# Token-layout turns on VectorE block transposes and GpSimd transfers, in place of TensorE transposes

## The chip, the cores and the metric

The kernel runs on one core of one Trainium2 chip. The metric is the device time of one execution in microseconds (us), median over several runs. A profile of one execution, taken by the hardware profiler, stands beside it. The engines are called TensorE (PE in the profile; its weight loads are PEld), VectorE (DVE), ScalarE (ACT), GpSimd (POOL) and SyncE (SP). SP, ACT and POOL issue DMA transfers.

## What is computed

A decoder block on 512 tokens of width 2048, all in float32: an attention and linear-attention mixer, a cross-attention over 256 memory tokens, and a SwiGLU feed-forward part of inner width 5632. The change lies in the last part:

```
x = x + concat(o_nsa, o_gla) @ w_out
x = x + cross_attention(rms_norm(x), rms_norm(mem)) @ w_co        # this x is "x2" below
hf = rms_norm(x, g_ffn)
gg, uu = split(hf @ w_gu, 2)
return x + (silu(gg) * uu) @ w_down                               # h = silu(gg) * uu
```

## The kernel before

Each float32 operand is split into a high and a low part, and each product is three matmuls: high by high, low by high, high by low. A split of a tile is a cast on ScalarE (`qh`, or the high part in a `PB` tile) and a subtraction on VectorE (`ql`, or the low part), both at line 159. The large products also use a scheme with seven block products in place of eight, so that sums and differences of blocks are formed first.

**Gate and up projections.** They run over 11 column groups n = 0 to 10. For n of 1 and more there are two phases: phase 1 with four of the seven products (`PHASE_1`), phase 2 with three (`PHASE_2`). In each phase a loop over kp = 0 to 7 loads a block of `w_gu` into one of three `raw` buffers (issued by SP), forms differences on VectorE (lines 1282, 1284, 1293), splits, and multiplies. `kept[kp]` holds a block from phase 1 for phase 2; these eight tiles have the tag `T2`, which has eight buffers in all. The dictionary `extra` hangs other work behind a kp. After phase 1, VectorE adds results out of PSUM (lines 1475 to 1479); after phase 2 it does so again (lines 1501 and 1503) and forms the four tiles `hs` of h for this n (lines 1508 and 1510). For n = 10 these come right at the end of the phase.

**Turning h.** `hs` has tokens on the partitions; the down projection needs h columns on the partitions. `turn(hs, n - 1, k)` is hung behind kp 2 and kp 4 of phase 2 of the next n. It makes eight TensorE transposes of 128x128 into two PSUM banks (line 1380), two ScalarE copies out of them (1383, 1384), four VectorE sums (1386 to 1389) in T2 tiles, and four stores to the DRAM tensor `hd` issued by ScalarE (line 1394). The two turns of n = 10 run inside step 0 of the down projection, behind its kp 2 and 4. There are 22 turns.

**Down projection.** Four steps, `STEPS`, over 44 blocks kp of `w_down`; step 0 uses one of the seven products, each other step two. h comes back from `hd` in six groups g0 to g5 of up to 1024 columns: `load_h` (line 1537, issued by GpSimd) into a `PB` tile, then a split (ACT cast, VectorE subtraction, line 159 with `PB`). g0 to g3 for step 0 are asked for just ahead of it.

**Residual.** x2 lies in DRAM with its features on the partitions. `turn_x2` turns it in step 0: 64 TensorE transposes (line 1604) in eight groups, 64 ScalarE copies out of PSUM (line 1607), four loads of 1 MB into a `raw` buffer. The fence `issue_after(turned ...)` in `load_w` holds later weight splits behind those copies.

**Other transfers of GpSimd** in these stages are paced by TensorE: sums of quarters of `w_down` made by accumulating DMAs (`td` at lines 144 and 146, `tw` at lines 1426 and 1428).

The order on each engine is that of a scheduler: it takes the program's order with priorities (`AHEAD`, `EVICT`), so a change moves rows on engines that the diff doesn't touch. DMAs issued by GpSimd rotate over eight semaphores, so each also waits for the one eight before it (waits named DMASW in the rows below; DMAHW are those of SP and ACT).

Of the kernel before, what the change touches and what calls it, by code (L numbers as in the profile page):

```python
# [17 lines left out]
T = 512  # L18
# [42 lines left out]
def hybrid_block(ctx: ExitStack, tc: tile.TileContext, x_t, mem_t, sv, cmat, umask, w_a, w_r67, w_v, w_vg, w_v3,  # L61
# [26 lines left out]
    def bank(tag):  # L88
        return psp.tile([128, 512], F32, name=tag, tag=tag, bufs={"mm": 3, "s": 2, "t": 2, "o": 1}[tag])
# [1282 lines left out]
    hd = [dram.tile([128, 7 * 512 * len(g)], F32, name="h", tag=f"h{g[0]}", bufs=1) for g in GRP]

    def turn(hs, n, k, tag="s"):
        def go():
            ps = [bank(tag), bank(tag)]
            for f in range(2):
                c = 256 * k + 128 * f
                for i in range(NT):
                    PE.transpose(ps[f][:, 128 * i:128 * i + 128], hs[i][:, c:c + 128], ident)  # L1380

            e, o, a, b = [sb1("T2") for _ in range(4)]
            S.copy(e, ps[0])
            S.copy(o, ps[1])
            x, y = slice(0, 256), slice(256, 512)
            V.tensor_sub(a[:, x], e[:, y], o[:, y])
            V.tensor_sub(b[:, x], e[:, x], e[:, y])
            V.tensor_sub(a[:, y], a[:, x], e[:, x])
            V.tensor_add(b[:, y], o[:, x], a[:, y])
            d = hd[n // 2].rearrange("q (p c) -> q p c", p=7)  # L1390
            c = 512 * (n % 2) + 256 * k
            S.dma_start(d[:, 0, c:c + 256], e[:, x])
            for p, t in ((1, o), (3, a), (5, b)):
                S.dma_start(d[:, p:p + 2, c:c + 256], t.rearrange("q (p c) -> q p c", p=2))
        return go

# [40 lines left out]
    def late_sum():  # L1437
        return {kp: [sums.pop(0)] for kp in (3, 5)}

    rc2 = []  # L1440
    gate = []
    hs = None
    fence = ()
    for n in range(NB):
        if n == 0:
            b1, bp = first_banks
            u, c11 = [sb2("C") for _ in range(2)], [sb2("C") for _ in range(2)]
            with tc.high_priority(offset=2 * EVICT):
# [84 lines left out]
    def load_h(step, g):  # L1533
        n = 512 * len(GRP[g])
        for a in STEPS[step]:
            raw = h_raw[a, g] = sb2("PB")
            i = G.dma_start(raw[:, :n], hd[g][:, a * n:a * n + n])
# [13 lines left out]
    def load_w(step, kp):  # L1551

        with tc.high_priority(offset=AHEAD):
# [14 lines left out]
            with ExitStack() as behind:  # L1568
                if (step, kp - 3) in turned:
                    behind.enter_context(tc.issue_after(turned[step, kp - 3].ins))  # L1570
                w = [split_cols(raw, 0, 1024)]
                if step % 2 and (step, kp) not in tw:
                    V.tensor_add(y, x, y)
                w.append(split_cols(raw, 1024, 1024))
# [16 lines left out]
    res, turned = {}, {}

    def turn_x2(m, raw):
        b, j = m // 8, m % 8 // 4
        if m % 8 == 0:
            res[1, b] = [sb1("T2") for _ in range(4)]
            if b:
                res[0, b] = [sb2("C") for _ in range(4)]
            else:
                res[0, b] = [sb2("PA") for _ in range(4)]  # L1600
        ps = bank("t")
        for i in range(NT):
            c = 512 * (m % 4) + 128 * i
            PE.transpose(ps[:, 128 * i:128 * i + 128], raw[:, c:c + 128], ident)  # L1604
        for i in range(NT):
            c = 128 * (m % 4)
            copied = S.copy(res[i // 2, b][2 * (i % 2) + j][:, c:c + 128], ps[:, 128 * i:128 * i + 128])
        return copied
# [29 lines left out]
    for step, plan in enumerate(STEPS):  # L1638
# [9 lines left out]
        for kp in range(NK):  # L1648
# [11 lines left out]
            elif 1 < kp < NK - 2:  # L1660
                for r in rs_:
                    down_product(step, r, kp, range(4))
            if step == 0 and kp % 2 and 5 <= kp < 21:
                for m in (kp - 5, kp - 4):
                    if m % 4 == 0:
                        raw = sb1("raw")
                        nc.sync.dma_start(raw, x2d[m // 4])
                    turned[step, kp] = turn_x2(m, raw)
            if step == 0 and kp in (2, 4):
                turn(hs, NB - 1, kp // 2 - 1, "t")()  # L1670
            if step == 0 and kp in (5, 11):
                load_h(0, len(GRP) - (2 if kp == 5 else 1))
            if step < 3 and kp % 4 == 3:
# [139 lines left out]
```

## Time and profile before

| | |
|---|---|
| median of 3 runs | 2294.36 us (2292.84 to 2295.81) |
| span of the profiled execution | 2291.5 us (the page gives no other time for that execution) |
| TensorE busy | 2280.9 us, 100% |
| VectorE, ScalarE, GpSimd busy | 1661.9 us (73%), 1183.2 us (52%), 164.0 us (7%) |
| instructions | 29538 |
| DMA | 434.17 MB, mean 189 GB/s; queue q0 (GpSimd) 17.6%, q1 (SP) 39.9%, q10 (ACT) 3.5% of sixteen engines' span |

The stages that the change touches lie at these times of the span: the pairs of phases for n = 1 to 10 up to 1857.97 us, and step 0 of the down projection from there to about 1922 us. A share in the table is of the whole span; the stages differ from it.

### The profile page before, as it was taken

To read this page: it belongs to the slowest core of one execution; us is meant where nothing else is said; L and a number is where in the kernel's file an instruction comes from. 1 tells how busy PE (TensorE), PEld (TensorE's weight loads), DVE (VectorE), ACT (ScalarE), POOL (GpSimd) and SP (SyncE) were. 2 spreads that over 40 slices of the span, in tenths; PEclk is the share of its full clock that TensorE was granted. 3 is DMA by queue.
4 is the path that set the end of the run, shared out by engine and by line. 5 is a ranking of instruction groups with operands and counts; after the bars stand their busy time and mean duration, and the time that the engine had idled before them with its cause. 6 is when DMAs were issued, how large, how long until landed. Compare 5 with 4: busy or idle time off the path is not lost.

```text
span 2291.5 us, 29538 instructions
## 1 busy us (share of the span) xinstructions
PE 2280.9 (100%) x10773; PEld 1894.0 (83%) x10773; DVE 1661.9 (73%) x2555; ACT 1183.2 (52%) x1855; POOL 164.0 (7%) x240
## 2 busy tenths in 40 slices
PE   9999999999999999999999999999999999999999
PEld 8988888888888888787888888888888888888887
DVE  6478766677774446698788788888887875775685
ACT  6334545566774345675455445454554565444452
POOL 0012100011110000110000000000000000000000
PEclk9999999999999999999999999999999999999999
DMA  6577656466655343685556656565665598766754
GB/s 197 140 187 182 173 156 173 122 172 174 164 168 173 132 135 138 215 235 175 178 180 201 185 163 200 184 191 159 204 201 165 163 329 292 268 239 250 265 206 147
DMA packets 140593, 434.17 MB, mean 189 GB/s; under 512 B 14464, under 2 KB 35200, under 8 KB 136992
## 3 DMA queue, kind: packets, MB, share of 16 engines
q1 hardware_dynamic: 80752, 306.83, 39.9%
q0 software_dynamic: 33824, 96.75, 17.6%
q10 hardware_dynamic: 25872, 28.71, 3.5%
q8 instruction: 84, 1.38, 0.2%
q14 instruction: 61, 0.50, 0.1%
HBM read 390.81 MB, written 94.11 MB: 212 GB/s over the span
## 4 chain that ended last, share of the span: by engine, by line
PE 94%; DVE 2%; DMA 2%; ACT 1%; issue 1%; SPq 0%; DVEq 0%; ACTq 0%
PE mm L99 51%; PE t L99 17%; PE s L99 14%; PE o L99 10%; DMA w<-w_c 1%; PE t L817 1%; PE s L1380 1%; DVE wl L159 1%; DMA w<-w_vsw 0%; ACT wh L159 0%; PE t L1604 0%; DVE ql L159 0%; DMA w<-w_a 0%; PE t L1071 0%; DMA P<-w_v 0%
## 5 line engine op out<-in xcount | busy, mean ns | idle before, releaser
L159 ACT CAST qh<-raw 128x1024 fp32r<-128x1024 f32 (+1 forms) x526 | 509.4, 981 | 473.4 <-PE t L99 120.6
L159 DVE TENSOR_TENSOR ql<-raw,qh 128x1024 fp32r<-128x1024 f32 (+1 forms) x526 | 589.3, 1130 | 137.6 <-PE mm L99 45.5
L99 PE MATMUL mm<-X,wh 128*128 128x512 f32 x1600 | 504.2, 395 | 0.0
L99 PEld LDWEIGHTS mm<-X,wh 128*128 128x128 f32 x1600 | 294.0, 188 | 56.4 <-issue 0.8
L99 PE MATMUL t<-qh,PB 128*128 128x512 f32 x968 | 335.3, 391 | 0.0
L99 PE MATMUL mm<-X,wl 128*128 128x512 f32 x800 | 313.6, 392 | 0.1
L99 PE MATMUL mm<-qh,PB 128*128 128x512 f32 x868 | 309.9, 390 | 1.8 <-ACT qh L159 0.9
L159 DVE TENSOR_TENSOR wl<-w,wh 128x1024 fp32r<-128x1024 f32 (+2 forms) x150 | 179.7, 1200 | 153.7 <-ACT wh L159 151.7
L159 ACT CAST wh<-w 128x1024 fp32r<-128x1024 f32 (+2 forms) x150 | 154.2, 1029 | 239.0 <-PE mm L99 176.8
L99 PE MATMUL s<-qh,PB 128*128 128x512 f32 x672 | 232.8, 391 | 0.7 <-ACT qh L159 0.7
L99 PE MATMUL mm<-qh,PA 128*128 128x512 f32 x640 | 221.6, 389 | 0.0
L99 PEld LDWEIGHTS t<-qh,PB 128*128 128x128 f32 x968 | 181.8, 188 | 37.3
L99 PEld LDWEIGHTS mm<-qh,PB 128*128 128x128 f32 x868 | 162.9, 188 | 37.0 <-ACT qh L159 2.1
L99 PE MATMUL t<-ql,PB 128*128 128x512 f32 x484 | 188.5, 389 | 0.1
L99 PE MATMUL o<-qh,PB 128*128 128x512 f32 x484 | 187.5, 389 | 0.0
L99 PEld LDWEIGHTS mm<-X,wl 128*128 128x128 f32 x800 | 150.2, 188 | 32.6 <-DVE wl L159 1.4
L99 PE MATMUL mm<-ql,PB 128*128 128x512 f32 x434 | 169.3, 390 | 0.0
L99 PEld LDWEIGHTS s<-qh,PB 128*128 128x128 f32 x672 | 126.1, 188 | 26.7 <-ACT qh L159 1.1
L99 PEld LDWEIGHTS mm<-qh,PA 128*128 128x128 f32 x640 | 120.1, 188 | 25.2
L99 PE MATMUL s<-ql,PB 128*128 128x512 f32 x336 | 131.3, 391 | 0.1
L99 PE MATMUL mm<-ql,PA 128*128 128x512 f32 x320 | 124.5, 389 | 0.0
L1282 DVE TENSOR_TENSOR raw<-raw 128x1024 f32<-128x1024 f32 x80 | 97.4, 1218 | 36.4 <-DMA raw<-w_gu 36.4
(501 smaller groups left out, 3448.7 us busy)
## 6 DMA issues: line engine op xcount, KB each, us to landing
raw<-w_gu SPq DMA_DIRECT2D x88, 768.0 KB, 4.4
raw<-w_gu SPq DMA_DIRECT2D x88, 512.0 KB, 3.6
raw<-w_down SPq DMA_DIRECT2D x84, 512.0 KB, 5.1
td<-w_down POOLq DMA_DIRECT2D x66, 512.0 KB, 6.3
w<-w_a SPq DMA_DIRECT2D x60, 512.0 KB, 4.5
raw<-td SPq DMA_DIRECT2D x22, 1024.0 KB, 4.8
PB<-h POOLq DMA_DIRECT2D x35, 512.0 KB, 5.9
h<-T ACTq DMA_DIRECT2D x66, 256.0 KB, 3.8
```

Source lines behind the costliest of these rows:

```text
L99: last_mm[0] = PE.matmul(*args, **kw)
L159: return S.copy(hi, src), V.tensor_sub(lo, src, hi)
L817: PE.transpose(tp[:, 128 * (i - j):128 * (i - j) + 128], ps_[b][:, POFF[i] + 128 * j:POFF[i] + 128 * j + 128], ident)
L1282: V.tensor_sub(raw[:, 0:1024], raw[:, 0:1024], raw[:, 512:1536])
L1380: PE.transpose(ps[f][:, 128 * i:128 * i + 128], hs[i][:, c:c + 128], ident)
```

## The change

1. **h is turned without TensorE.** `turn` returns two functions. `go` makes, on VectorE, four transposes of 32x32 blocks (one instruction each, 128 partitions by 8 blocks of 32) and the same four sums. Since only the inside of each 32x32 block is turned, the blocks still have to be moved to their places; `put` does that with sixteen GpSimd DMAs into `hd`, whose pieces are 64 elements (256 bytes) long. `go` hangs behind kp 2 and 4 of phase 2, `put` behind kp 3 and 5; both follow in step 0 for n = 10. The two PSUM banks and copies and the ACT stores are gone.
2. **x2 is turned ahead of the down projection.** `x2_turn` does it in 16 tiles of 128x512, one in a phase: `x2_load` (GpSimd, into the only buffer of tag `hT`) and, behind kp 6, `x2_blocks` (one VectorE block transpose in place); `x2_store` (four GpSimd DMAs of 32x16x32 in pieces of 128 bytes, into the new DRAM tensor `x2n`) comes in the next phase behind kp 2, ahead of the next load. In step 0, `load_x2` takes it back with 64 SP loads of 32x512. `turn_x2`, its 64 transposes and its 64 copies are gone, and so is the fence in `load_w`.
3. **Token order.** Block transposes give the tokens another order, and the output rows come in it; they are put in order outside of the device time.

```diff
-    def turn(hs, n, k, tag="s"):
+    def x2_load(m):
+            x2_tiles[m] = sb2("hT")
+            G.dma_start(x2_tiles[m], x2d[m // 4][:, 512 * (m % 4):512 * (m % 4) + 512])
+    def x2_blocks(m):
+            V.transpose(x2_tiles[m], x2_tiles[m])
+    def x2_store(m):
+            rows = x2n.rearrange("(b r) f -> r b f", r=32)
+            for a in range(4):
+                p = slice(32 * a, 32 * a + 32)
+                c = 128 * m + 32 * a
+                G.dma_start(rows[:, :, c:c + 32], x2_tiles[m][p].rearrange("r (b c) -> r b c", c=32))
+    def turn(hs, n, k):
         def go():
-            ps = [bank(tag), bank(tag)]
-            for f in range(2):
-                c = 256 * k + 128 * f
-                for i in range(NT):
-                    PE.transpose(ps[f][:, 128 * i:128 * i + 128], hs[i][:, c:c + 128], ident)
-            e, o, a, b = [sb1("T2") for _ in range(4)]
-            S.copy(e, ps[0])
-            S.copy(o, ps[1])
+            x, y, a, b = [sb1("T2") for _ in range(4)]
+            for i in range(NT):
+                to = (x, y)[i // 2].rearrange("q (g i c) -> q g i c", i=2, c=32)
+                V.transpose(to[:, :, i % 2], hs[i][:, 256 * k:256 * k + 256].rearrange("q (g c) -> q g c", c=32))
...
-            S.dma_start(d[:, 0, c:c + 256], e[:, x])
-            for p, t in ((1, o), (3, a), (5, b)):
-                S.dma_start(d[:, p:p + 2, c:c + 256], t.rearrange("q (p c) -> q p c", p=2))
+        def put():
+            for q in range(4):
+                p = slice(32 * q, 32 * q + 32)
+                d = hd[n // 2].rearrange("(g r) c -> r g c", r=32)[:, :, c + 64 * q:c + 64 * q + 64]
+                G.dma_start(d[:, 8:12], y[p, 256:].rearrange("r (g c) -> r g c", c=64))
+                for i, z in ((0, x), (12, a), (20, b)):
+                    G.dma_start(d[:, i:i + 8], z[p].rearrange("r (g c) -> r g c", c=64))
+        return go, put
...
+    def x2_turn(extra):
+        m = next(turns, None)
+        if m is not None:
+            if m:
+                extra.setdefault(2, []).append(x2_store(m - 1))
+            if m < KT:
+                extra.setdefault(2, []).append(x2_load(m))
+                extra.setdefault(6, []).append(x2_blocks(m))
...
-            extra = {2: [turn(hs, n - 1, 0)], 4: [turn(hs, n - 1, 1)], 6: [lambda: gate.append(last_mm[0])]}
+            (go0, put0), (go1, put1) = [turn(hs, n - 1, k) for k in range(2)]
+            extra = {2: [go0], 3: [put0], 4: [go1], 5: [put1], 6: [lambda: gate.append(last_mm[0])]}
...
-            if step == 0 and kp % 2 and 5 <= kp < 21:
-                for m in (kp - 5, kp - 4):
-                    if m % 4 == 0:
-                        raw = sb1("raw")
-                        nc.sync.dma_start(raw, x2d[m // 4])
-                    turned[step, kp] = turn_x2(m, raw)
+            if step == 0 and kp in (6, 8, 10, 12):
+                load_x2(*((0, 1), (1, 1), (0, 0), (1, 0))[kp // 2 - 3])
             if step == 0 and kp in (2, 4):
-                turn(hs, NB - 1, kp // 2 - 1, "t")()
+                go, put = turn(hs, NB - 1, kp // 2 - 1)
+                go()
+                put()
```

The scheduler moves rows at three places. In the rows, numbers behind a name are buffers, and square brackets hold the semaphores that the row waits for.

**VectorE at the seam between phase 2 of n = 10 and step 0.** Before, the split of g0 (the row with `PB_16128`, the low part of g0) stands in the middle of phase 2, ahead of the sums (L1386) of the turn of n = 9:

```order
L159 TENSOR_TENSOR ql_15944<-raw_15936,qh_15943 128x512 [waits PE_49,Activation_49]
L1293 TENSOR_TENSOR raw_16018<-raw_16018,T2_15706 128x512 [waits DMAHW6_49,DVE_49]
L159 TENSOR_TENSOR ql_15969<-raw_15965,qh_15968 128x1024 [waits PE_49,Activation_49]
L159 TENSOR_TENSOR PB_16128<-PB_16125,PB_16127 128x1024 [waits DMASW4_49,Activation_49]
L159 TENSOR_TENSOR ql_15973<-raw_15965,qh_15972 128x512 [waits DVE_49,PE_49]
L1293 TENSOR_TENSOR raw_16047<-raw_16047,T2_15745 128x512 [waits DMAHW7_49,DVE_49]
L1386 TENSOR_TENSOR T2_15924<-T2_15922,T2_15923 128x256 [waits Activation_49]
L159 TENSOR_TENSOR ql_16022<-raw_16018,qh_16021 128x1024 [waits PE_49]
```

After, both turns of n = 10 stand at the seam, and the split of g0 (`PB_16321`) comes behind them, with that of g1 (`PB_16327`) next:

```order
L1408 TENSOR_TENSOR T2_16402<-T2_16402,T2_16400 128x256 [waits DVE_49]
L1404 STREAM_TRANSPOSE T2_16475<-C_16298 128x8x32 [waits DMASW4_49,DMASW0_49]
L1409 TENSOR_TENSOR T2_16403<-T2_16400,T2_16402 128x256 [waits DVE_49]
L1404 STREAM_TRANSPOSE T2_16475<-C_16299 128x8x32
L1404 STREAM_TRANSPOSE T2_16476<-C_16300 128x8x32 [waits DMASW5_49,DMASW1_49]
L1404 STREAM_TRANSPOSE T2_16476<-C_16301 128x8x32
L1406 TENSOR_TENSOR T2_16477<-T2_16476 128x256 [waits DMASW6_49,DMASW2_49,DVE_49]
L1408 TENSOR_TENSOR T2_16477<-T2_16477,T2_16475 128x256 [waits DVE_49]
L1407 TENSOR_TENSOR T2_16478<-T2_16475,T2_16476 128x256 [waits DMASW7_49,DMASW3_49]
L1409 TENSOR_TENSOR T2_16478<-T2_16475,T2_16477 128x256 [waits DVE_49]
L159 TENSOR_TENSOR PB_16321<-PB_16318,PB_16320 128x1024 [waits DMASW4_49,Activation_49]
L159 TENSOR_TENSOR PB_16327<-PB_16324,PB_16326 128x1024 [waits DMASW0_49,Activation_49]
```

The split of g0 moved from phase 2 to behind all of phase 2's results, the four rows that form `hs`, and the eight transposes and eight sums of n = 10's turns.

**GpSimd at the same seam.** Before, the loads of g0 to g3 follow the last `td` sum:

```order
L146 DMA td_93<-w_down 128x1024 [waits PE_49]
L144 DMA td_93<-td_93 128x2x512 [waits DMASW3_49,DMASW2_49,PE_49]
L1537 DMA PB_16125<-h_8854 128x1024 [waits DMAHW3_49,DMAHW4_49,PE_49,Pool_49]
L1537 DMA PB_16131<-h_8855 128x1024 [waits DMAHW3_49,DMAHW4_49,DMASW5_49,PE_49]
L1537 DMA PB_16137<-h_8856 128x1024 [waits DMAHW3_49,DMASW4_49,DMAHW4_49,DVE_49,PE_49]
L1537 DMA PB_16143<-h_8857 128x1024 [waits DMAHW3_49,DMASW7_49,DMAHW4_49,DMASW5_49,DVE_49]
```

After, the load of g0 (`PB_16318`) comes behind the 32 transfers of `put` of n = 9's turns, the last of which are the first five rows here, and the loads of g1 and on stand between those of n = 10:

```order
L1420 DMA h_8858<-T2_16186 32x8x64 [waits DMASW7_49]
L1418 DMA h_8858<-T2_16184 32x4x64 [waits DMASW0_49]
L1420 DMA h_8858<-T2_16183 32x8x64 [waits DMASW1_49]
L1420 DMA h_8858<-T2_16185 32x8x64 [waits DMASW2_49]
L1420 DMA h_8858<-T2_16186 32x8x64 [waits DMASW3_49]
L1576 DMA PB_16318<-h_8854 128x1024 [waits DMASW4_49,PE_49,Pool_49]
L1418 DMA h_8859<-T2_16401 32x4x64 [waits DMASW5_49,DVE_49]
L1420 DMA h_8859<-T2_16400 32x8x64 [waits DMASW6_49]
L1420 DMA h_8859<-T2_16402 32x8x64 [waits DMASW7_49,DVE_49]
L1576 DMA PB_16324<-h_8855 128x1024 [waits DMASW0_49,PE_49]
L1420 DMA h_8859<-T2_16403 32x8x64 [waits DMASW1_49,DVE_49]
```

The loads of h moved behind the puts, and share their eight semaphores.

**VectorE and GpSimd between phase 1 and phase 2 of a middle group.** Before, VectorE goes from the splits of phase 2's first block straight to the additions out of PSUM (L1475):

```order
L1293 TENSOR_TENSOR raw_10222<-raw_10222,T2_9915 128x512 [waits DMAHW2_49]
L159 TENSOR_TENSOR ql_10215<-raw_10211,qh_10214 128x1024 [waits PE_49,Activation_49]
L159 TENSOR_TENSOR ql_10219<-raw_10211,qh_10218 128x512 [waits PE_49,Activation_49]
L1475 TENSOR_TENSOR C_10199<-C_10199,s_9887 128x512 [waits PE_49,Activation_49]
L159 TENSOR_TENSOR ql_10226<-raw_10222,qh_10225 128x1024 [waits DVE_49,PE_49]
L1475 TENSOR_TENSOR C_10200<-C_10200,s_9888 128x512 [waits PE_49,Activation_49]
L1477 TENSOR_TENSOR C_10201<-C_10199,t_9889 128x512 [waits DVE_49,PE_49]
L1477 TENSOR_TENSOR C_10202<-C_10200,t_9890 128x512 [waits DVE_49,PE_49]
```

After, the block transpose of the second x2 tile of the pair (`hT_10964`) stands ahead of them (now L1513):

```order
L1404 STREAM_TRANSPOSE T2_10949<-C_10514 128x8x32 [waits DVE_49]
L1404 STREAM_TRANSPOSE T2_10949<-C_10515 128x8x32
L159 TENSOR_TENSOR ql_10865<-raw_10861,qh_10864 128x1024 [waits PE_49,Activation_49]
L159 TENSOR_TENSOR ql_10869<-raw_10861,qh_10868 128x512 [waits PE_49,Activation_49]
L1384 STREAM_TRANSPOSE hT_10964<-hT_10964 128x512 [waits DMASW3_49,DMASW2_49,DMASW6_49,DMASW1_49,DMASW0_49]
L1513 TENSOR_TENSOR C_10849<-C_10849,s_10530 128x512 [waits PE_49,Activation_49]
L159 TENSOR_TENSOR ql_10876<-raw_10872,qh_10875 128x1024 [waits DVE_49,PE_49]
L1513 TENSOR_TENSOR C_10850<-C_10850,s_10531 128x512 [waits PE_49,Activation_49]
L1515 TENSOR_TENSOR C_10851<-C_10849,t_10532 128x512 [waits DVE_49,PE_49]
```

On GpSimd, that tile's load stands behind the four stores of the tile before it (`hT_10654`, the same single buffer), a `td` sum, and the first transfer of a put, which itself waits for VectorE (the transposes `T2_10949` above):

```order
L1379 DMA hT_10654<-x2_8866 128x512 [waits DMAHW0_49,DMASW5_49]
L1452 DMA tw_9400<-w_down 256x512 [waits DMASW6_49,DMASW4_49]
L146 DMA td_85<-w_down 128x1024 [waits DMASW7_49,PE_49]
L1393 DMA x2n_8860<-hT_10654 32x16x32 [waits DMASW0_49,DVE_49]
L1393 DMA x2n_8860<-hT_10654 32x16x32 [waits DMASW1_49]
L1393 DMA x2n_8860<-hT_10654 32x16x32 [waits DMASW2_49]
L1393 DMA x2n_8860<-hT_10654 32x16x32 [waits DMASW3_49]
L144 DMA td_85<-td_85 128x2x512 [waits DMASW7_49,PE_49]
L1418 DMA h_8854<-T2_10949 32x4x64 [waits DMASW5_49,DVE_49]
L1379 DMA hT_10964<-x2_8866 128x512 [waits DMASW3_49,DMASW6_49,DMASW2_49,DMAHW3_49,DMASW1_49,DMASW0_49]
L1420 DMA h_8854<-T2_10948 32x8x64
```

Nothing of this stood on GpSimd in these phases before but the rows of `td` and `tw`.

More of the change, by code (lines that the diff above doesn't have):

```diff
@@ L1371, in hybrid_block @@
     GRP = [range(g, min(g + 2, NB)) for g in range(0, NB, 2)]
[L1372 to L1374 removed]
+    hd = [dram.tile([7 * 128, 512 * len(g)], F32, name="h", tag=f"h{g[0]}", bufs=1) for g in GRP]
+    x2n = dram.tile([T, D], F32, name="x2n", tag="x2n", bufs=1)
+    x2_tiles = {}
+    def x2_load(m):
         def go():
[L1376 to L1395 removed]
@@ new lines, in turn, with go @@
+    def turn(hs, n, k):
+        t = []
+        def go():
+            x, y, a, b = [sb1("T2") for _ in range(4)]
+            for i in range(NT):
+                to = (x, y)[i // 2].rearrange("q (g i c) -> q g i c", i=2, c=32)
+                V.transpose(to[:, :, i % 2], hs[i][:, 256 * k:256 * k + 256].rearrange("q (g c) -> q g c", c=32))
+            e, o = slice(0, 256), slice(256, 512)
+            V.tensor_sub(a[:, e], y[:, e], y[:, o])
+            V.tensor_sub(b[:, e], x[:, e], y[:, e])
+            V.tensor_sub(a[:, o], a[:, e], x[:, e])
+            V.tensor_add(b[:, o], x[:, o], a[:, o])
+            t.extend((x, y, a, b))
+        def put():
+            x, y, a, b = t
+            c = 512 * (n % 2) + 256 * k
+            for q in range(4):
[5 more added lines that the diff above has]
+        return go, put
@@ L1438, in late_sum @@
         return {kp: [sums.pop(0)] for kp in (3, 5)}
+    turns = iter(range(KT + 1))
+    def x2_turn(extra):
[6 more added lines that the diff above has]
+                extra.setdefault(6, []).append(x2_blocks(m))
+        return extra
     rc2 = []
@@ L1493, in hybrid_block @@
         else:
-            phase(lambda kp: weights_2(n, kp), (b1, b2, b3), PHASE_2, (1, 0, 2), (0, 1, 2), False, AHEAD, extra,
-                  (fa, fv))
+            phase(lambda kp: weights_2(n, kp), (b1, b2, b3), PHASE_2, (1, 0, 2), (0, 1, 2), False, AHEAD,
+                  x2_turn(extra), (fa, fv))
         g1, g2 = [sb2("C") for _ in range(2)], [sb2("C") for _ in range(2)]
@@ L1536, in load_h @@
             raw = h_raw[a, g] = sb2("PB")
-            i = G.dma_start(raw[:, :n], hd[g][:, a * n:a * n + n])
+            i = G.dma_start(raw[:, :n], hd[g][128 * a:128 * a + 128])
             if step == 0 and g in (2, 3):
@@ L1567, in load_w @@
                 nc.sync.dma_start(y, tw.get((3, kp), td[kp][:, 1024:]))
[L1568 to L1574, printed above, removed]
+            w = [split_cols(raw, 0, 1024)]
+            if step % 2 and (step, kp) not in tw:
+                V.tensor_add(y, x, y)
+            w.append(split_cols(raw, 1024, 1024))
             if step == 2:
@@ L1588, in down_product, with load_x2 @@
                 start=fresh and kp == 0, stop=kp == NK - 1, again=not fresh)
[L1591 to L1608, printed above, removed]
+    res = {}
+    def load_x2(a, b):
+        res[a, b] = [sb1("T2") if a else sb2("C" if b else "PA") for _ in quad]
+        for (i, j), t in zip(quad, res[a, b]):
+            for q in range(4):
+                r, c = 256 * a + 64 * i + 32 * (q // 2) + 128 * (q % 2), 1024 * b + 512 * j
+                nc.sync.dma_start(t[32 * q:32 * q + 32], x2n[r:r + 32, c:c + 512])
     def store(x, a, b):
@@ L1811 @@
     r = run_bass_kernel_spmd(nc, [arrays], core_ids=[0])
-    return r.results[0]["out_0_dram"].reshape(1, T, D)
+    y = r.results[0]["out_0_dram"].reshape(2, 2, 2, 2, 32, D)
+    return y.transpose(0, 3, 1, 2, 4, 5).reshape(1, T, D)
```

12 lines of the change are left out of this document (9 added, 3 removed).

## The prediction

> **What bounds the kernel now.** I read the engine shares first, then the clock row and the chain of work that ended last.
>
> ```profile
> PE 2280.9 (100%) x10773; PEld 1894.0 (83%) x10773; DVE 1661.9 (73%) x2555; ACT 1183.2 (52%) x1855; POOL 164.0 (7%) x240
> PEclk9999999999999999999999999999999999999999
> PE 94%; DVE 2%; DMA 2%; ACT 1%; issue 1%; SPq 0%; DVEq 0%; ACTq 0%
> ```
>
> TensorE is busy for the whole span and its granted clock is full in every slice. The waits of TensorE say how close its suppliers come. The longest wait:
>
> ```profile
> PE t L99 <- DVE ones_r L229: 1.5, 1, 1.5
> ```
>
> So whatever leaves TensorE shortens the run, as long as no supplier becomes late; and whatever makes a supplier late lengthens it one for one. The forecast is a gain on TensorE less the new lateness. Everything is summed on the profiled span of 2291.5 us, which is 2.9 below the median of 2294.36; I carry the difference over to the median.
>
> **What leaves TensorE.** One group of eight transposes in TensorE's timeline (start, duration, then the work):
>
> ```profile
> 1131.72 0.39 PE L99 MATMUL o<-qh,PB 128*128 128x512 f32 x1
> 1131.95 1.03 PE L1380 MATMUL s<-ident,C 128*128 128x128 f32 x8
> 1132.74 0.48 PE L99 MATMUL t<-qh,PB 128*128 128x512 f32 x1
> 1133.06 0.40 PE L99 MATMUL t<-ql,PB 128*128 128x512 f32 x1
> ```
>
> Durations overlap, so starts count. Matmuls start 0.23 apart (1131.72, 1131.95). The group holds TensorE from 1131.95 to 1132.74, 0.79 us, and the matmul behind it takes 0.32 instead of 0.23: 0.88 a group. The counts:
>
> ```profile
> L1380 PE MATMUL s<-ident,C x160: 270/272/273, 1132.0 to 1845.6; 128*128 128x128 f32 x160
> L1380 PE MATMUL t<-ident,C x16: 270/272/273, 1866.1 to 1873.2; 128*128 128x128 f32 x16
> L1604 PE MATMUL t<-ident,raw x64: 270/273/273, 1876.1 to 1921.3; 128*128 128x128 f32 x64
> ```
>
> 240 transposes are 30 groups: 30 x 0.88 = **26.4 us** of gain, 17.6 in the gate-up phases and 8.8 in step 0. With them go ScalarE's copies and stores; ScalarE is 52% busy, so I cost that at nothing.
>
> The Trainium skill, "VectorE: DVE Perf Modes", section "The three transpose paths", gives 390 ns for a TensorE transpose of 128x128 in bf16 and 311 for VectorE's. The row shows 0.79 us for eight, about 0.1 each once pipelined, so that by the page's 390 the removal would be worth 240 x 0.39 = 94 us; the trace decides for 26.4.
>
> **Loss 1: the first split of step 0.** VectorE's order after the change puts the split of g0 behind the end of phase 2, the rows that form h, and both turns of n = 10. TensorE's third matmul of step 0 needs that split. Before:
>
> ```profile
> 1837.23 1.23 DVE L159 TENSOR_TENSOR PB<-PB 128x1024 fp32r<-128x1024 f32 x1 [1.97 <-ACT PB L159]
> ...
> 1859.06 0.68 DVE L1503 TENSOR_TENSOR C<-C,o 128x512 f32<-128x512 f32 x1
> 1859.66 1.22 DVE L159 TENSOR_TENSOR ql<-raw,qh 128x1024 fp32r<-128x1024 f32 x1
> 1860.80 1.41 DVE L1508 SCALAR_TENSOR_TENSOR C<-C,rc 128x512 f32<-128x512 f32 x2
> 1862.12 0.74 DVE L1510 SCALAR_TENSOR_TENSOR C<-C,rc 128x512 f32<-128x512 f32 x1
> ...
> 1871.01 0.42 DVE L1386 TENSOR_TENSOR T<-T,T 128x256 f32<-128x256 f32 x1 [1.01 <-ACT T L1384]
> 1871.36 0.42 DVE L1387 TENSOR_TENSOR T<-T 128x256 f32<-128x256 f32 x1
> 1871.69 0.42 DVE L1388 TENSOR_TENSOR T<-T,T 128x256 f32<-128x256 f32 x1
> 1872.14 0.42 DVE L1389 TENSOR_TENSOR T<-T,T 128x256 f32<-128x256 f32 x1
> ```
>
> ```profile
> 1857.97 0.39 PE L99 MATMUL s<-qh,PB 128*128 128x512 f32 x1
> 1858.19 0.39 PE L99 MATMUL s<-ql,PB 128*128 128x512 f32 x1
> 1858.42 0.62 PE L99 MATMUL s<-qh,PB 128*128 128x512 f32 x2
> ```
>
> Before, the split ran at 1837.23, 21 us ahead of its use. Now count from 1857.97, where TensorE leaves phase 2. VectorE ends the additions at 1859.66 (+1.69), one `ql` (+1.14), four rows forming h at 0.66 (+2.64), then eight transposes and eight sums of 128x256. The trace has no block transpose; the nearest row of its size, a sum of 128x256, starts 0.34 apart, 0.45 where it needs the one before (1871.69 to 1872.14). Lower end 0.2 each, upper 0.66 (the 128x512 row); I take the sum's own 0.34, with some waits: 16 x 0.34 + 4 x 0.11 = 5.9. Then the split, 1.14. Together 1.69 + 1.14 + 2.64 + 5.9 + 1.14 = 12.5 after 1857.97, and TensorE stands from 0.45 on: **12.0 us** lost, with ends of 11 and 14.6 (transposes at 0.2 or 0.66). Here more than the saving in step 0 (8.8) is lost. What is queued behind the wait is only the rest of step 0; weights are loaded in the meantime, so nothing else becomes late. The load of g0 itself stands on GpSimd behind a put of 16, and would have to be over 10 us later than phase 2's end to decide.
>
> A wait of 12 us is eight times the longest that TensorE had, so no row here shows the clock after one. The Trainium skill, "TensorE: Matmul & The Clock Gate", section "What's actually happening", states half rate for about 3.4 us after an idle window of that length; by the page the sum would be 1.7 us longer, which is inside the range.
>
> **Loss 2: the x2 tiles between phases 1 and 2.** For n of about 2 to 8 the second tile's transpose stands ahead of the additions that free PSUM for phase 2:
>
> ```profile
> 1183.07 0.68 DVE L1293 TENSOR_TENSOR raw<-raw,T 128x512 f32<-128x512 f32 x1
> 1188.48 0.69 DVE L1293 TENSOR_TENSOR raw<-raw,T 128x512 f32<-128x512 f32 x1 [2.46 <-DMA raw<-w_gu]
> 1194.72 0.69 DVE L1475 TENSOR_TENSOR C<-C,s 128x512 f32<-128x512 f32 x1 [1.57 <-ACT C L1474]
> 1197.06 1.28 DVE L1477 TENSOR_TENSOR C<-C,t 128x512 f32<-128x512 f32 x2
> ```
>
> ```profile
> 1200.57 0.39 PE L99 MATMUL t<-qh,PB 128*128 128x512 f32 x1
> ```
>
> The last addition for `t` ends at 1198.3 and is needed at 1200.57; with the rows between, the transpose must be over by about 1197.3. The first tile's transpose runs behind L1293 of 1183.07, to 1184.5. Then GpSimd issues four stores, each of 512 pieces; the last must have landed before the one `hT` buffer is loaded again, and the load must land. Durations of issues, and times to landing (a store of `spill`, and a 128x512 load `PA<-x`):
>
> ```profile
> L144 POOL DMA_DIRECT2D td<-td x22 | 26.0, 1184 | 163.1 <-PE s L99 93.1 <-PE mm L99 57.6 <-issue 12.4
> L1428 POOL DMA_DIRECT2D tw<-w_down x8 | 4.1, 514 | 288.0 <-PE o L99 288.0
> L1537 POOL DMA_DIRECT2D PB<-h x42 | 22.4, 535 | 324.6 <-PE mm L99 141.7 <-DVE PB L159 52.6 <-PE t L99 44.7
> ```
>
> ```profile
> DMA to landing us min/median/max: 2.4/4.8/7.9
> ```
>
> ```profile
> DMA to landing us min/median/max: 3.2/4.6/6.6
> ```
>
> An issue of 128 pieces takes 0.535, the `td` row of 256 pieces 1.18. For 512 pieces: 0.54 if pieces don't matter, 2.46 on a line through both rows. I take 1.18, the row that also has a three-dimensional pattern. Last store issued at 1184.5 + 3 x 1.18 = 1188.0, landed 1192.8, load landed 1197.4, transposed (0.65) 1198.05: 0.75 late. With 0.54: not late. With 2.46: last store 1191.9, landed 1196.7, load landed 1201.3, done 1202: 4.7 late. Times seven pairs: **0, 5 or 33 us**; I take 5.
>
> **Loss 3: transfers.** A pair gets 7168 pieces of 256 bytes (two puts, 3584 each) and 4096 of 128 (eight stores), and loses the ACT stores, 1920 packets.
>
> ```profile
> q10 hardware_dynamic: 25872, 28.71, 3.5%
> ```
>
> ```profile
> 1154.10:1197.60 43.50, 43.50 (x193) 35.80 (x192) 36.01 (x41) 21.98 (x28) 1.72 (x2) 1.00 0.58 178
> 1197.60:1232.00 34.40, 34.40 (x161) 28.64 (x160) 26.06 (x38) 15.93 (x21) 1.67 (x2) 1.00 0.57 189
> 1280.00:1358.00 78.00, 78.00 (x354) 64.71 (x353) 63.53 (x80) 39.18 (x50) 3.13 (x4) 1.00 0.61 186
> 1230.00:1235.00 5.00, 4.35 (x19) 3.30 (x19) 5.00 (x8) 3.71 (x6) 0.98 (x1) 1.00 1.00 231
> ```
>
> The ACT queue's packets of 1.1 KB cost 3.5% of 16 x 2291.5 over 25872, 49.6 ns. At that price per piece the pair gains (11264 - 1920) x 0.0496 / 16 = 29 us per DMA engine, and the share of 0.58 (last but one column; the rows are phase 1, phase 2, a whole pair and a crowded stretch, with the window, TensorE, its loads, VectorE, ScalarE, GpSimd, clock, share and GB/s) goes to 0.96; by bytes (11.4 and 5.7 ns) it stays where it is. In between, at 30 and 25 ns: share 0.76. The last row shows what fullness costs: at share 1.00 TensorE stood 0.65 of 5 us. I take a fifth of a microsecond to 0.4 a pair, **2 us** for eight pairs; ends 0 and 10 (two such places a pair). VectorE gets 8 x 0.34 + 2 x 0.6, 4 us more a pair on 36.01 of 43.5 and 26.06 of 34.4; it stays under its limit, so this costs nothing beyond the places named.
>
> The Trainium skill, "DMA: Bandwidth & Descriptors", section "Why small descriptors are slow (HBM only)", counts 256/32 + 3 = 11 cycles for a piece of 256 bytes, a quarter of it overhead; by the page loss 3 would vanish, as by bytes. No row here has such pieces in number.
>
> **The sum.** -26.4 + 12.0 + 5 + 2 = -7.4; on the median 2294.36 - 7.4 = **2287 us**. The bound for telling a change of this kernel is 0.2%, 4.6 us: faster is under 2289.8, slower over 2298.9.
>
> **The rivals.**
> - *Short waits.* VectorE turns at 0.2 a piece, stores are issued at 0.54, small pieces go by bytes: losses 11 + 0 + 0, and 2294.4 - 15.4 = 2279. For it: the flat 0.51 to 0.54 of most GpSimd issues. Should the seam cost less than counted, by VectorE working ahead, down to 2270. Chance 0.22.
> - *The single hT buffer holds up every pair.* It ends on the other side: at 2.46 a store, 4.7 x 7 = 33 in place of 5, so 2315. It decides from a store issue of about 1.9, where the sum turns to loss over 0.2%. For it: 1184 against 535 as pieces double. Against: the accumulating rows, of which that one is, may be dearer for another reason. Chance 0.17.
> - *Full DMA engines.* Pieces at 49.6 ns, share 0.96: weights late at two or more places a pair, 10 to 20 us: -7.4 + 13 = +6, 2300. For it: the 0.65 at share 1.00. Chance 0.13.
> - *Nothing is saved*, since other waits fill TensorE's place: that needs suppliers with no slack, and TensorE's waits are under 1.5 us; 0.03, near 2294.
>
> The likeliest case, the sum, has 0.45 and reaches from 2280 to 2297: two thirds faster than 0.2%, the rest same. Faster: 0.22 + 0.29 = 0.51; slower: 0.17 + 0.10 = 0.27 and a little of the sum's, 0.28; same 0.21. The range takes in short waits from 2273 and the single buffer to 2316.
>
> **What would show it.** Lines 1380 and 1604 gone, and TensorE busy some 26 us less. A wait of TensorE at the start of step 0 of about 12 us on `PB` from VectorE, the longest in its list. At the seams of seven pairs, a wait on `C` of under 1 us, and VectorE's idle time ahead of L1384 put down to `hT`'s load. GpSimd's issue at L1393 near 1.2 us decides between the sum and the single buffer; DMA share in the pairs near 0.75 between the sum and full engines. I would be wrong if the seam wait is under 8 us, or if any pair takes longer than its 78 us.

## The result: slower, by what looked like a rival

The changed kernel takes 2315.36 us (median of 4 runs, 2314.8 to 2319.99) against 2294.06 before: 21.3 us more. The ratio as estimated from all runs is 1.0099, interval 1.0084 to 1.0113; the two medians alone give 1.0093. The forecast was 2287 and faster. The profiled execution took 2314.8, its span is 2313.0, 21.5 over that of before. (A detail of the text above: a step of the down projection has 22 kp, not 44.)

The page of the changed kernel, with the engine row, the clock row and the DMA queue of GpSimd:

```profile
PE 2270.6 (98%) x10533; PEld 1870.0 (81%) x10533; DVE 1697.6 (73%) x2659; ACT 1152.6 (50%) x1747; POOL 417.8 (18%) x672
PEclk9999999999999999999999999999999989999999
q0 software_dynamic: 48416, 125.35, 21.7%
```

The 240 transposes are gone (10773 to 10533), but TensorE now idles 42.4 us of its span in place of 10.6. Its waits, by line:

```profile
PE mm L99 <- DVE ql L159: 9.9, 6, 2.2
PE s L99 <- DVE PB L159: 8.7, 2, 8.2
PE s L99 <- ACT qh L159: 6.1, 7, 1.1
PE s L99 <- ACT PB L159: 5.0, 2, 2.9
PE t L99 <- DVE ql L159: 2.9, 6, 0.5
```

None of the five was there before but 0.7 of the third. By stage (from the first matmul of phase 2 of one n to that of the next, read in TensorE's timeline; the column of both_sp belongs to an experiment below):

| | before | after | both_sp |
|---|---|---|---|
| phase 2 of n = 1 to that of n = 2 | 78.1 | 76.9 | 76.3 |
| the next seven pairs, one by one | 79.3, 78.0, 78.0, 78.4, 78.0, 78.0, 78.0 | 81.9, 80.7, 79.6, 81.1, 80.5, 80.2, 80.6 | 76.2 to 76.7 |
| n = 9 to n = 10 | 78.0 | 76.8 | 76.2 |
| from step 0's start to the end | 433.5 | 442.3 | 433.7 |

Two pairs gained 1.2 to 1.3 us of the 1.8 that their transposes cost. Seven pairs that should have come down to 76.2 went to 80.7 in the mean: 7 x 4.5 = 31 us lost. From step 0 on, 8.8 us should have gone and 8.8 came: 17.6 lost. Together -26.4 + 31 + 17.6 = 22, against 21.5 measured.

**A seam of such a pair.** GpSimd and VectorE of the changed kernel (start, duration, engine, line, work, and in brackets the idle time ahead and what ended it):

```profile
1183.43 2.61 POOL L1393 DMA_DIRECT2D x2n<-hT  x4 [7.42 <-DVE hT L1384]
1186.35 1.19 POOL L144 DMA_DIRECT2D td<-td  x1 [0.32 <-PE s L99]
1191.84 0.59 POOL L1418 DMA_DIRECT2D h<-T  x1 [4.30 <-DVE T L1404]
1192.53 0.56 POOL L1379 DMA_DIRECT2D hT<-x  x1
```

```profile
1182.43 0.70 DVE L1384 STREAM_TRANSPOSE hT<-hT 128x512 f32<-128x512 f32 x1
1189.04 0.69 DVE L1293 TENSOR_TENSOR raw<-raw,T 128x512 f32<-128x512 f32 x1 [3.01 <-DMA raw<-w_gu]
1190.78 0.76 DVE L1404 STREAM_TRANSPOSE T<-C 128x256 f32<-128x256 f32 x2
1191.47 1.78 DVE L159 TENSOR_TENSOR ql<-raw,qh 128x1024 fp32r<-128x1024 f32 x2
1198.07 0.71 DVE L1384 STREAM_TRANSPOSE hT<-hT 128x512 f32<-128x512 f32 x1 [4.81 <-DMA h<-T]
1198.70 0.65 DVE L1513 TENSOR_TENSOR C<-C,s 128x512 f32<-128x512 f32 x1
1199.27 1.21 DVE L159 TENSOR_TENSOR ql<-raw,qh 128x1024 fp32r<-128x1024 f32 x1
```

The four stores are out in 2.6 us. The load of the next tile leaves at 1192.53, behind a put's first transfer that waited for the block transposes of 1190.78, which had stood behind a subtraction waiting for weights. It lands 5.4 us later; VectorE stands idle 4.81 at the transpose and comes to its next `ql` at 1199.27. (The bracket names a put's transfer as releaser, the last event of several; the transpose needs the tile.) TensorE, in the changed kernel's timeline:

```profile
1200.54 0.69 PE L99 MATMUL mm<-ql,PA 128*128 128x512 f32 x1 [2.03 <-DVE ql L159]
1201.03 1.06 PE L99 MATMUL mm<-qh,PA 128*128 128x512 f32 x2
1201.88 0.63 PE L99 MATMUL mm<-ql,PA 128*128 128x512 f32 x1
...
1204.29 0.39 PE L99 MATMUL t<-ql,PB 128*128 128x512 f32 x1
```

A wait of 2.03 us, then starts 0.43 apart in place of 0.23 for some 3 us: about 1.7 us more (the granted clock is halved there, see the clock rows below). Where phase 1 starts, a wait of 1.14 on a cast follows (1236.08). This pair lost 5.7 us in all.

The pairs are not alike in this. Adding up by how much the starts of TensorE's matmuls lie more than 0.227 apart, the seven pairs lost 18.6 us at the seams (0.8 to 4.1 each), 10.8 where phase 1 starts, and 2 elsewhere. Of the 18.6, 3.4 are the halved clock, which came in two of the seven (from 1200.7 and 1282.6).

**The seam into step 0.**

```profile
1864.80 0.58 POOL L1576 DMA_DIRECT2D PB<-h  x1
1873.55 1.40 DVE L1547 SCALAR_TENSOR_TENSOR C<-C,rc 128x512 f32<-128x512 f32 x2
1876.20 1.41 DVE L1404 STREAM_TRANSPOSE T<-C 128x256 f32<-128x256 f32 x4
1881.92 1.22 DVE L159 TENSOR_TENSOR PB<-PB 128x1024 fp32r<-128x1024 f32 x1
```

```profile
1873.78 0.80 PE L99 MATMUL s<-qh,PB 128*128 128x512 f32 x1 [2.90 <-ACT PB L159]
1883.19 1.22 PE L99 MATMUL s<-qh,PB 128*128 128x512 f32 x2 [8.19 <-DVE PB L159]
1930.31 0.50 PE L99 MATMUL s<-qh,PB 128*128 128x512 f32 x1 [2.08 <-ACT PB L159]
```

TensorE left phase 2 at 1870.7 and went on at 1883.19, 12.5 us later, as worked out. The wait of 2.08 for g4's cast wasn't foreseen. The clock rows (window, four engine columns and GpSimd, granted clock, DMA share, GB/s):

```profile
1200.00:1210.00 10.00, 9.46 (x35) 7.70 (x36) 10.00 (x17) 3.28 (x4) 2.08 (x4) 0.83 0.36 105
1883.00:1893.00 10.00, 9.81 (x36) 7.94 (x37) 4.07 (x5) 4.05 (x5) 8.88 (x17) 0.81 0.83 257
1930.00:1940.00 10.00, 9.16 (x33) 7.21 (x34) 5.86 (x5) 4.79 (x6) 1.06 (x2) 0.83 0.82 252
```

The last two lost 1.9 and 1.7 us. 12.0 + 2.6 (the wait for g4 and 0.5 behind it) + 3.6 = 18.2, about the 17.6 that are missing.

### The profile page after: what moved, and what is told of

Read it like the earlier page. It is cut to its first block, busy times and chain, and to the rows that moved or that the text cites. A ratio compares the mean times of both kernels' runs of the same rounds, so it can differ in the third digit from the quotient of the medians.

```text
span 2313.0 us, 29742 instructions
## 1 busy us (share of the span) xinstructions
PE 2270.6 (98%) x10533; PEld 1870.0 (81%) x10533; DVE 1697.6 (73%) x2659; ACT 1152.6 (50%) x1747; POOL 417.8 (18%) x672
## 2 busy tenths in 40 slices
DMA packets 136566, 442.60 MB, mean 191 GB/s; under 512 B 20928, under 2 KB 21952, under 8 KB 133472
## 5 line engine op out<-in xcount | busy, mean ns | idle before, releaser
L1420 POOL DMA_DIRECT2D h<-T x264 | 154.0, 590 | 154.5 <-DVE T L1408 112.0
```

The lines of the kernel that those rows point to most:

```text
L1420: G.dma_start(d[:, i:i + 8], z[p].rearrange("r (g c) -> r g c", c=64))
```

## Experiments

Theory A: what loses is order in queues. VectorE, in order, stands at a transpose whose tile is late, and GpSimd's loads stand behind puts. Theory B: transfers in small pieces, and their number, make weights late. Expectations were written with the numbers above in view; "2294" and so on are medians. Each ratio is to the kernel before, measured again beside the run (medians 2292.33 to 2294.76); a difference to the changed kernel's 2315 compares separate measurements and is good to some 2 us.

**1. x2_sp: x2 loads on SyncE.**

```diff
-            G.dma_start(x2_tiles[m], x2d[m // 4][:, ...
+            nc.sync.dma_start(x2_tiles[m], x2d[m // 4][:, ...
```

> The sixteen loads of x2 tiles are issued by SyncE instead of GpSimd; everything else is the changed kernel. Theory A (one queue): the seven seams between phase 1 and phase 2 lose because the load of the second x2 tile stands on GpSimd behind the first transfer of a put, which waits for VectorE. Then its wait goes (2.0 us and 0.5 us behind it, with the half-rate clock after it, about 3 us a pair): 7 x 3 = 21 us less than 2315, about 2294, no TensorE wait over 1.3 us between 1190 and 1690 us. Theory B (traffic): small pieces fill the DMA engines and make the weights late, whoever issues the load: 2312 to 2317, waits unchanged.

Measured 2286.46; ratio to before 0.9972, interval 0.9961 to 0.9984: 29 us less than the changed kernel, nearly all that the pairs had lost, since the wait of 1.1 us at phase 1's start went too. TensorE's only long waits were those of step 0. The x2 loads and the places of the transposes:

```profile
DMA to landing us min/median/max: 2.5/4.2/6.6
1181.69 0.70 DVE L1384 STREAM_TRANSPOSE hT<-hT 128x512 f32<-128x512 f32 x1
1208.20 0.67 DVE L1384 STREAM_TRANSPOSE hT<-hT 128x512 f32<-128x512 f32 x1
```

VectorE never idled ahead of one. This run changes two things at once: the queue, and with it VectorE's order. The second transpose of a pair is no longer ahead of the additions at the seam but some 12 us into phase 2. So it shows that the loss is in the x2 chain and not in traffic as such (the same bytes moved), but not which of its links.

**2. h0_sp: the loads of g0 to g3 for step 0 on SyncE.**

```diff
-            i = G.dma_start(raw[:, :n], hd[g][128 * a:128 * a + 128])
+            i = (nc.sync if step == 0 and g < 4 else G).dma_start(raw[:, :n], hd[g][128 * a:128 * a + 128])
```

> The four loads of h groups g0 to g3 for step 0 are issued by SyncE instead of GpSimd; the rest is the changed kernel. Theory A: the load of g0 is late since it stands behind the puts, and that lets the scheduler place its split behind both turns of n = 10. In this kernel's order the split stands in phase 2 again, so the TensorE waits of 2.9 and 8.2 us and the low clock after them go: 13 us less, about 2302; the pairs keep their 80 us. Theory B: the weights are late at step 0 from the traffic of the puts, so a wait of several us stays: 2309 or more.

Measured 2306.15, ratio 1.0063 (1.0046 to 1.0081): 9 less, not 13. Both waits at the seam are gone; the wait for g4's cast grew from 2.1 to 12.4:

```profile
PE s L99 <- ACT PB L159: 12.4, 1, 12.4
```

**3. both_sp: 1 and 2 together.**

> Both of these: x2 loads and the first four h loads on SyncE. Theory A: the gains add up, 2315 - 21 - 13 = 2281, that is faster than before by 13 us; what is left of the pairs' loss is the wait of 1.1 us where phase 1 starts. Theory B: little more than one of them alone, 2300 or more. A third way: SyncE's own queue of weight loads is held up by loads that wait for stores; then new waits of TensorE on casts of weights appear, and the time is over 2290.

Measured 2275.1, ratio 0.9931 (0.9915 to 0.9948). The gains add up (29 + 9 = 38; 40 measured). All nine pairs take 76.2 to 76.7 us. What is left is in step 0: 9.0 us over the 424.7 that before's 433.5 less 8.8 would give, with a wait of 7.24 for a cast of h. Its load left on GpSimd at 1878.61 and landed 8.8 us later, at 1887.4; the casts that ScalarE, in order, made first held it up for only 0.8 more (the first row merges three loads, the second is the landing of the first of them):

```profile
1878.61 1.63 POOL L1576 DMA_DIRECT2D PB<-h  x3
DMA to landing us min/median/max: 8.8/8.8/8.8
1888.26 1.04 ACT L159 CAST PB<-PB 128x1024 fp32r<-128x1024 f32 x1
```

**4. turn_only: h the new way, x2 as before.** `turn`, `put` and `load_h` of the changed kernel in the kernel before.

> Only h is turned the new way; x2 is turned by TensorE in step 0 as before (the residual is added in the old token order, the sums of the output are not the reference's). Theory A: without x2 tiles the seams are free, and 22 groups of transposes are saved, 19 us; in its order the split of g0 stands in phase 2. With 1.1 us a pair left at the start of phase 1 (8 us): about 2283. Theory B (the puts' 256-byte pieces are what costs): pairs stay near 80 us and the time is 2300 or more.

Measured 2285.44, ratio 0.9969 (0.9959 to 0.9979); pairs at 76.2 to 77.2, so the puts' transfers cost almost nothing there, less than the 1.1 us expected.

**5. x2_only: x2 the new way, h as before.**

> Only x2 is turned the new way, with its loads on GpSimd; h is turned by TensorE as before, so nothing of a put stands on GpSimd (x2 comes in another token order than h, the sums of the output are not the reference's). Theory A: no wait at the seams, pairs at 78.0 as before; step 0 saves 8 groups, 7 us: about 2287. Theory B (the x2 chain with its one buffer costs by itself): 4 us a pair lost, about 2312.

Measured 2309.09, ratio 1.0063 (1.0047 to 1.008). I expected 2287; theory B's 2312 is near by its number, but it had 4 us in every pair. Without puts in GpSimd's queue the scheduler packed the x2 chain into fewer pairs, which then took 81.4, 90.1 and 88.4 us, and the others 78.0. VectorE stood at transposes there:

```profile
1201.63 0.71 DVE L1384 STREAM_TRANSPOSE hT<-hT 128x512 f32<-128x512 f32 x1 [4.20 <-DMA hT<-x]
1243.67 0.71 DVE L1384 STREAM_TRANSPOSE hT<-hT 128x512 f32<-128x512 f32 x1 [2.76 <-DMA hT<-x]
1289.29 0.71 DVE L1384 STREAM_TRANSPOSE hT<-hT 128x512 f32<-128x512 f32 x1 [2.83 <-DMA hT<-x]
```

So a put ahead of the load isn't needed for a loss of this kind: the chain through one buffer (store, land, load, land) does it alone.

**6. put_x_first: a put sends x before y.**

```diff
-                G.dma_start(d[:, 8:12], y[p, 256:].rearrange("r (g c) -> r g c", c=64))
                 for i, z in ((0, x), (12, a), (20, b)):
                     G.dma_start(d[:, i:i + 8], z[p].rearrange("r (g c) -> r g c", c=64))
+                G.dma_start(d[:, 8:12], y[p, 256:].rearrange("r (g c) -> r g c", c=64))
```

> The changed kernel, all on GpSimd as there, but each put sends x before y. The load of the second x2 tile still stands on GpSimd behind a put's first transfer, but that one now needs the first two block transposes (over at about 1185 us) and not the last two (1191.5). Theory A (what stands ahead of the load in the queue waits): the load goes out some 3 us earlier and the seam waits of 2.0 us and the low clock behind them are gone: 7 x 3.5 = 25 less, about 2290. Theory B (GpSimd's loads land late, or small pieces crowd the engines): no change, 2312 to 2318. The step 0 wait stays in both.

Measured 2301.94, ratio 1.0038 (1.0023 to 1.0053): 13 less, half of what A expected, and not where A expected it. The put no longer waits, but the stores start 1.3 us later, and now their landing holds the load, which leaves at nearly the same time as before (1192.27, 1192.53 in the changed kernel):

```profile
1184.77 2.60 POOL L1393 DMA_DIRECT2D x2n<-hT  x4 [6.81 <-DVE hT L1384]
1189.03 1.08 POOL L1419 DMA_DIRECT2D h<-T  x1
1192.27 0.58 POOL L1379 DMA_DIRECT2D hT<-x  x1 [2.16 <-DMA x2n<-hT]
1196.86 0.71 DVE L1384 STREAM_TRANSPOSE hT<-hT 128x512 f32<-128x512 f32 x1 [2.79 <-DMA h<-T]
```

In the changed kernel the last store had landed at 1191.15 and the put left at 1191.84: two waits end 0.7 us apart, and taking one away leaves the other. TensorE's waits in this run:

```profile
PE mm L99 <- DVE ql L159: 8.9, 7, 2.2
PE s L99 <- ACT qh L159: 0.9, 1, 0.9
```

The first row, the waits at the seams, was 9.9 in the changed kernel and is nearly all still there (the 2.9 on `t` behind them are down to 0.6). The second was 6.1; its six waits at the starts of phase 1 are gone, and most of the 13 us came from there. So a late start of phase 1 doesn't simply follow from a late seam, and what made it late in the changed kernel stays open.

**7. no_odd: every second x2 transpose left out.**

```diff
-            V.transpose(x2_tiles[m], x2_tiles[m])
+            if m % 2 == 0:
+                V.transpose(x2_tiles[m], x2_tiles[m])
```

> The changed kernel with every second of the sixteen block transposes of x2 left out (those tiles are loaded and stored unturned, so half of the residual isn't turned); all transfers stay, all on GpSimd. If the seams lose because VectorE, in order, stands at a transpose whose tile hasn't landed, and the additions out of PSUM behind it: no such wait where no second tile is, pairs at 76.3, about 2315 - 29 = 2286. If transfers as such (their number, their landing, GpSimd's time) make weights late: the pairs stay at 80, about 2312. The wait at step 0 stays in both.

Measured 2289.12, ratio 0.9986 (0.9976 to 0.9995); pairs 76.2 to 77.5, but 78.1 for the first. All loads and stores are still on GpSimd, all pieces still move. So transfers as such are not the loss; VectorE standing in order at the transpose ahead of the additions is what is missing here. (The scheduler moved GpSimd's rows as well: the x2 loads nearest to that of 1192.53 in the changed kernel leave at 1178.10 and 1204.06, so the same transfers run at other times.)

**8. x2_act: x2 loads on ScalarE.**

> As x2_sp, but the x2 loads are issued by ScalarE. If it matters only that the loads leave GpSimd's queue, where they stand behind puts: as x2_sp, 2286 within 4 us. If SyncE's queue was the point: some of the gain is missing, 2295 or more; ScalarE waits in order too, and a load that waits for stores holds up the casts behind it.

Measured 2287.33, ratio 0.9977 (0.9967 to 0.9987), as x2_sp. So it doesn't matter that the loads go to SyncE, only that they leave GpSimd's queue. VectorE's order moved here too: the second transpose of a pair comes some 12 us into phase 2 (1209.8 after 1197.15), so neither run tells the queue from the order.

**9. put_twice: each put writes twice** (on all_sp, below; `for dst in (hd, hd2)` around its transfers).

> As all_sp, but each put writes its sixteen transfers twice, the second time to tensors that nothing reads: 32 transfers and 7168 pieces of 256 bytes more in a pair. If small pieces are what limits (the forecast's loss 3 at 50 ns a piece): 7168 x 0.05 / 16 = 22 us of all engines more in a pair, full engines, and 10 us or more lost. If they cost by bytes and GpSimd has room (about 37 us of issues in a pair of 76): within 3 us of all_sp, about 2267 to 2270.

Measured 2327.71, ratio 1.0148 (1.013 to 1.0166), 53 more than all_sp: the loss is far over 3 us, yet the engines are not full. GpSimd's DMA queue in all_sp and then in put_twice, and one pair of the latter:

```profile
q0 software_dynamic: 46336, 118.27, 20.9%
```

```profile
q0 software_dynamic: 57600, 138.48, 23.8%
1354.00:1433.00 79.00, 76.85 (x329) 62.77 (x329) 64.39 (x85) 32.99 (x41) 45.53 (x77) 0.98 0.75 219
1431.25 1.22 DVE L1282 TENSOR_TENSOR raw<-raw 128x1024 f32<-128x1024 f32 x1 [8.18 <-DMA raw<-w_gu]
```

The 22 x 3584 = 78848 more pieces made 11264 more packets, half of them under 512 bytes (26560 such packets on the page, 20928 in all_sp). They took (0.238 x 2330.9 - 0.209 x 2271.1) x 16 = 1281 us of engine time, 16 ns a piece. The DMA share in the pair is 0.75. What went wrong looks like order again: three copies into `kept` tiles ran late and together (1421.72 on ScalarE), `raw` buffers came free late, and weights were waited for 8.18 us. Since `kept` and the turns share the eight T2 tiles, twice the transfers hold them about twice as long; that this is the reason is argued from the order, not shown by a run of its own. 31 us went in step 0, in waits for casts of h, whose loads read what the puts write.

**10 to 12. The rest of step 0.** all_sp issues g4 and g5 on SyncE too.

> As both_sp, but the loads of g4 and g5 for step 0 are issued by SyncE too. Theory A: the wait of 7.2 us that both_sp has in step 0 is for the cast of g4, whose load stands on GpSimd behind the 32 transfers of n = 10's puts; it goes, with the low clock after it: 2275 - 8 = 2267, which is 2294 less the 26.4 us of transposes. If SyncE's weight loads are held up by the h loads instead, waits on casts of weights appear in step 0 and the time stays over 2273.

Measured 2274.49, ratio 0.9917 (0.9902 to 0.9932): the same as both_sp. The wait for g4 went, waits of 2.0 and less on weights came. x2_spread moved three quarters of the x2 loads into step 1.

> As all_sp, but the 64 loads of turned x2 don't all stand in step 0: a quarter at kp 10 of step 0, the others at kp 4, 9 and 14 of step 1. In all_sp they stand on SyncE ahead of weight loads for up to 8 us at a time, and casts wait for weights (TensorE lost 2.5 us there, with a granted clock of 0.84 behind it). If that is what is left in step 0: 2274.5 - 4 = 2270. If the loads are the same hindrance in step 1, no change.

Measured 2279.82, ratio 0.9942 (0.9927 to 0.9957), 5 more. The hypothesis fell: g5's load then stood on SyncE behind x2 loads, and TensorE waited 5.6 us for its cast. x2_t2_late hung only the x2 loads into T2 tiles later in step 0.

> As all_sp, but the x2 loads into T2 tiles, whose buffers the turns of n = 10 hold until GpSimd's puts have landed, are hung behind kp 15 and 18 of step 0 in place of 8 and 12; in this kernel's order on SyncE the weight loads of kp 16 to 21 stand ahead of them. If the rest of the loss in step 0 is SyncE standing at T2 loads ahead of weight loads: TensorE's waits on casts between 1885 and 1905 us go, 2274.5 - 5 = 2269. If it is the DMA engines, whose share is 0.9 to 1.0 there in all versions: no change, 2272 to 2278.

Measured 2273.8, ratio 0.9909 (0.9893 to 0.9926): no difference to all_sp; TensorE still lost some 5 us in small waits around 1900. Each order of these loads trades one wait for another, with a DMA share near 1.0 there:

```profile
1892.00:1902.00 10.00, 8.00 (x30) 6.12 (x29) 5.46 (x5) 5.40 (x6) 0.53 (x1) 0.84 1.03 354
```

(That is all_sp.) Whether bytes or order set the last 4 to 9 us of step 0 stays open. The three best versions, both_sp, all_sp and x2_t2_late, can't be told apart; all are 0.7 to 0.9% faster than before.

## Why the prediction was wrong

- **The gain of 26.4 us** was right: in both_sp a pair is 1.8 us shorter and TensorE is busy for 25.9 us less (2255.0). In the changed kernel its busy time fell by only 10.3, part of which is the halved clock, and the two pairs without seam waits came down by 1.2 to 1.3.
- **Loss 1 (12.0 us) was right** in place, reason and size: 12.0 of wait, two matmuls in between. Block transposes cost what the row of their size did: 1.41 for four, 0.34 apart. "Nothing else becomes late" was wrong: g4 lost 2.6, which h0_sp turned into 12.4. The half-rate clock was left to a sentence on the Trainium skill, "TensorE: Matmul & The Clock Gate" ("What's actually happening"); its 1.7 us came true behind the wait of 8.19, with 1.9. The second loss of that size, 1.7 from 1930 on, followed a wait of 2.08, too short for what the sentence says.
- **Loss 2 is the step that failed**: 5 us was forecast for the seven pairs, 31 came. Two things were wrong in it.
  - *The lateness of the tile.* The stores were cheaper than the row taken for them (0.65 for 512 pieces, not 1.18), but the load left at 1192.5 all the same: I had let the stores' landing alone decide (1192.8) and taken the put's first transfer as ready, where it waited for VectorE until 1191.8. The load's landing took 5.4, not 4.6. From the end of the first tile's transpose to that of the second it was 15.6 us (1183.1 to 1198.7), not 13.5 (1184.5 to 1198.05). And I took the time of need from the kernel before. In the changed kernel phase 2 starts 1.1 us earlier (1196.76, not 1197.85), and TensorE waits first not for the additions on `C` but for the `ql` that stands behind the transpose and one addition: it could have used it at 1198.35 and went on at 1200.54. That is 2.2 us late, where 0.75 was forecast.
  - *What else such a row costs.* I counted lateness one for one, and only at the seam. The seams cost 18.6 us, of which 3.4 are the halved clock in two of them. Another 10.8 came where phase 1 starts, which the forecast put at nothing. These went with the seam waits in x2_sp and no_odd, but also in put_x_first, where the seam waits stayed, so their cause is open. In a list of rows in order, a transpose 4.8 us ahead of its tile is a stop for everything behind it.
- **Loss 3** (2 us): in both_sp no pair is more than 0.5 us over the 76.2. Pieces cost 16 ns each, nearer to the 11.4 by bytes than to the 30 taken; the Trainium skill, "DMA: Bandwidth & Descriptors" ("Why small descriptors are slow (HBM only)"), gives 11 cycles, which makes an estimate of 13 ns if they are cycles of the 850 MHz fabric clock in its section "Where 436 GB/s comes from"; the trace's 16 is a quarter above that. The packets are not the pieces: a transfer of 256 pieces made 32 packets, half of them small.
- **The rival "the single hT buffer holds up every pair"** had 2315 and 0.17, and came out at 2315.4. Its place was right and its reason was not: it rested on stores at 2.46 us, and they took 0.65. It had 33 us at the seams, where 18.6 came; the rest of the time was lost at the starts of phase 1 and in step 0, where it had nothing beyond loss 1. That its number fits is luck, and no evidence for its working.

## What to carry to other kernels

A chain of store, landing, load and landing through one buffer took 14.5 us in the changed kernel (1183.43 to 1197.94) and 12.0 in put_x_first, and in a program whose engines run in order its last instruction stops all that stands behind it; look for what stands right behind, and move the load to a queue where nothing ahead of it waits. Moving the x2 loads and four loads of h off GpSimd's queue turned +1.0% into -0.7%, with the same transposes and the same bytes. Where TensorE is the bound, price a wait of 2 us not at 2 but at 2 to 4: the halved clock added 1.7 in two of seven seams. And work out when a row is needed from the new order and the new times, not from those before.

## What the runs showed of the hardware

- The granted clock halves for whole stretches of 3.41 us. In the changed kernel they start at 1200.68, 1282.60, 1873.11 and 1931.13, which are 24, 173 and 17 times 3.413 us apart, so a span can be laid out in such windows. Two windows of the changed kernel, each with the one behind it (columns as in the clock rows above):

```profile
1197.27:1200.68 3.41, 1.38 (x7) 0.84 (x6) 2.61 (x4) 0.75 (x1) 1.61 (x3) 1.00 0.32 96
1200.68:1204.09 3.41, 3.41 (x9) 2.67 (x10) 3.41 (x7) 0.00 (x0) 0.32 (x1) 0.50 0.19 38
1439.61:1443.02 3.41, 1.68 (x8) 1.06 (x7) 3.05 (x5) 0.60 (x1) 1.94 (x3) 1.00 0.35 94
1443.02:1446.44 3.42, 2.89 (x13) 1.97 (x12) 3.42 (x6) 0.00 (x0) 0.00 (x0) 1.00 0.10 20
```

  TensorE is idle for 2.03 us of the first, and the next runs at half rate; for 1.73 of the third, and the next runs at full rate. Over the 14 traces of this case, all 28 windows at full rate with 1.74 us or more of idle time were followed by a halved one, and none with 1.56 or less; of the three between, that with 1.57 was, those with 1.68 and 1.73 were not. So about half a window of idle time is what counts, and with it where a wait falls: the wait of 2.01 that ends at 1604.32 lies across two windows, with 1.14 and 0.87 idle, and halved nothing. The Trainium skill, "TensorE: Matmul & The Clock Gate" ("What's actually happening"), names an idle window of about 3.4 us that runs freely. The traces agree with its length and that it runs freely, but half of one idle was enough.
- GpSimd's issue time hardly depends on the pieces: 0.56 for 128, 0.59 for 256, 0.65 for 512. The 1.18 of the `td` rows belongs to something else in them; they accumulate, but no run here shows that this is why.
